# Gathers queued in two parts around the gate matrix, and low halves in two GpSimd instructions

## The chip, the cores and the metric

The kernel runs on one core of a Trainium2 chip. The metric is the device time of one execution in microseconds (us). The engines are called PE (TensorE, with PEld for its weight loads), DVE (VectorE), ACT (ScalarE), POOL (GpSimd) and SP (SyncE, which issues plain DMAs here). Each engine works through its own queue in order. A line number such as L820 is the line of the kernel before.

## What is computed

One decoder layer over 1024 tokens of width 1024, all in float32: a norm, one combined projection, three token mixers merged by gates (the mixer), and then a feed-forward part in which every token chooses 128 of 16384 experts. Only that last part is touched by the gathers:

```python
def peer_ffn(xn, w_peer_q, peer_keys, peer_u, peer_v):      # per block of tokens
    sc = jnp.einsum('thid,hikd->thik', q, peer_keys)         # scores for two halves of the key
    top_v, top_i = lax.top_k(sc, PEER_TOPK)
    ...
    eid = jnp.take_along_axis(cidx, best_pos, axis=-1)       # 8 heads x 16 experts for each token
    gate = jax.nn.softmax(best_v, axis=-1)
    u = peer_u[eid]
    act = jax.nn.gelu(jnp.einsum('thkd,td->thk', u, xt))
    v = peer_v[eid]
    return jnp.einsum('thk,thkd->td', gate * act, v)
x = x + peer_ffn(rms_norm(x, ln_ffn))                        # then a final norm
```

## The kernel before

**Tiling.** Tokens lie on 128 partitions. The 1024 tokens go in three blocks (`BLOCKS`): 256, 512 and 256. `mixer` is a generator for one block; while block b finishes, the first steps of block b+1 run between, and `routing` (which finds `eid` and `gate`) of block b runs beside them. For the middle block the experts are computed densely (`dense`, with `gate_matrix` making a 512 x 16384 matrix of gates from one-hot `quad` tiles, `g_d`). For the other two blocks, four tiles of 128 tokens, the experts' rows are fetched: `gathered` issues for each tile 128 gathers from `u` and 128 from `v`, 1024 in all. A gather (L820) is an indirect DMA, issued by GpSimd, of 128 rows of 4 KB into a buffer `g4{k % 7}`; VectorE then multiplies a `u` row tile with the tokens and sums (L830, result in `dots`), or adds a weighted `v` row tile to the output rows in PSUM (L837).

**Weights.** Every weight tile of 128 x 1024 goes through `unit`: SP loads `raw`, ScalarE rounds it to `whi` (L164), and GpSimd, for some units VectorE, makes the rest `wlo = raw - whi` (L165, in `split`). TensorE then multiplies three times (`mm3`, L191 to L193). So a unit is 24 matmuls and one subtraction.

**Order.** The program text is traced once, and a planner then orders each engine's instructions by priority and by a timeline of its own, before the run; the order is fixed on the chip. Buffers of one name (`tag`) are handed out in the order of the program text. `unit` notes in `marks` its priority, its ScalarE and GpSimd instructions and a rate. `pace` turns the rates into due times: `due` adds up the rates, a slot of due time is two gathers, and the gather takes the priority of its unit (`cur_priority`) and is queued on GpSimd behind that unit's subtraction (`issue_after`, L819). The rates are 1.0 and 0.3 in the first and second routing (`RATE_ROUTING`), 1.5 and 0.5 in the mixers behind them (`RATE_MIXER`), 0.5 from the last routing on (`RATE_LAST`), and 0 from the dense stage on; there the gathers that are left are spread evenly over the dense units.

**Buffers.** There are seven gather buffers (`NG`, tags `g40` to `g46`). `gate_matrix` takes its quads from three of them, tags `g44` to `g46` (L856), and one more use of `g46`. While the gate matrix is made, `slots` lets gathers use only the other four (`NQ_GATHER`). The loop that traces all gathers (`for t in range(TT)`, at the end of `layer_kernel`) comes last in the program text.

Of the kernel before, what the change touches and what calls it, by code (L numbers as in the profile page):

```python
# [8 lines left out]
F32 = mybir.dt.float32  # L9
# [5 lines left out]
ALU = mybir.AluOpType  # L15
# [3 lines left out]
D = 1024  # L19
# [3 lines left out]
TT = T // P  # L23
# [13 lines left out]
SLOTS = HEADS * TOPK  # L37
# [6 lines left out]
NG = 7  # L44
# [6 lines left out]
NQ_GATHER = 4  # L51
# [12 lines left out]
def layer_kernel(ctx, tc, a, out_d):  # L64
    nc = tc.nc
# [97 lines left out]
    def split(hi, lo, src, eng=None):  # L163
        return (nc.scalar.copy(hi, src),  # L164
                (eng or nc.vector).tensor_tensor(lo, src, hi.bitcast(F32), op=ALU.subtract))  # L165

    marks, rate = [], [0.0]
# [3 lines left out]
    def unit(src, n=D, k=KD):  # L171
        prio = tc.cur_priority
        if in_mix[0] and len(marks) % 4 == 3:
            raw = tmp.tile([P, D], F32, tag="raw4", name="raw", bufs=1)
        else:
            raw = wts.tile([P, D], F32, tag="raw", name="raw")
        dst = raw[:, :n]
        if len(src.shape) == 3:
            dst = dst.rearrange("p (k c) -> p k c", k=src.shape[1])
        nc.sync.dma_start(dst, src)  # L180
        hi = wts.tile([P, D], F32R, tag="whi", name="whi")
        lo = wts.tile([P, D], F32R, tag="wlo", name="wlo")
        share[0] += lo_dve[0]
        on_dve = share[0] >= 1
        share[0] -= on_dve
        first, second = split(hi[:, :n], lo[:, :n], raw[:, :n], nc.vector if on_dve else nc.gpsimd)
        marks.append((prio, first, marks[-1][2] if on_dve and marks else second, rate[0]))
        return (hi[:, :n].rearrange("p (k c) -> p k c", k=k), lo[:, :n].rearrange("p (k c) -> p k c", k=k))

# [613 lines left out]
    def held(src):  # L803

        stage = gat.tile([P, D], F32, tag="held", name="stage", bufs=1)
        nc.sync.dma_start(stage, src)
        ps = psum.tile([P, D], F32, tag="row", name="row_ps", bufs=1)
        nc.scalar.copy(ps, stage)
        return ps

    def gathered(tt, eid, gt, pace, slots):

        def rows_of(table, k, half):
            n = tt * SLOTS + (half * SLOTS + k) / 2
            m0, m1 = pace(n), pace(n, LAG)
            if m0:
                tc.cur_priority = m0[0]
            g = gat.tile([P, D], F32, tag=f"g4{k % slots(n)}", name="g4", bufs=1)
            with (tc.issue_after(m0[2].ins) if m0 else nullcontext()):  # L819
                nc.gpsimd.indirect_dma_start(out=g, out_offset=None, in_=a[table],  # L820
                                             in_offset=bass.IndirectOffsetOnAxis(ap=eid[:, k:k + 1], axis=0))
            if m0:
                tc.cur_priority = m1[0]
            return g, m1

        xn = held(xn_d[tt * P:(tt + 1) * P, :])
        w = gat.tile([P, SLOTS], F32, tag="dots", name="dots", bufs=2)
        for k in range(SLOTS):
            g, m1 = rows_of("u", k, 0)
            nc.vector.scalar_tensor_tensor(g, g, 1.0, xn, op0=ALU.mult, op1=ALU.mult, accum_out=col(w, k))  # L830
        with (tc.issue_after(m1[1].ins) if m1 else nullcontext()):
            nc.scalar.activation(w, w, AF.Gelu_apprx_tanh)
        nc.vector.tensor_tensor(w, w, gt, op=ALU.mult)
        acc = held(x2_d[ROW0[tt]:ROW0[tt] + P, :])
        for k in range(SLOTS):
            g, _ = rows_of("v", k, 1)
            nc.vector.scalar_tensor_tensor(acc, g, col(w, k), acc, op0=ALU.mult, op1=ALU.add)  # L837
        final_rows(tt, acc)
# [125 lines left out]
    eid = gat.tile([P, TT, SLOTS], I32, tag="eid", name="eid", bufs=1)  # L964
# [13 lines left out]
    def fill(count, dp=None):  # L978
        for _ in range(count):
            if todo:  # L980
                i, n = todo.pop(0)
                act = d2(dp) if dp else tmp.tile([P, T], F32, tag="sp", name="sp", bufs=2)
                nc.sync.dma_start(act_d[n], dense_act(i, held_xT[0], None, act, mm_ps()))

    mT = mem_norm()
    x_sb = x_norm(0)
    mem_kv(mT)
    now = mixer(0, x_turn(x_sb, PK_LN_MIX))
    for b in range(1, len(BLOCKS)):
# [6 lines left out]
        shared = []  # L996
# [31 lines left out]
        for _ in range(chunks):  # L1028
            until(nxt, "chunk")
            spill(KD // chunks)  # L1030
    m_gate = len(marks)
    quads = gate_matrix(ij_dense, gate_dense)
    gates_done = False
    for label in now:
# [8 lines left out]
                pass  # L1043
        elif not isinstance(label, str):
            xnT = label
    m_gathers = len(marks)
    rate[0] = RATE_LAST
    routing(xnT, b16()[:, 0:2048], gate[:, 2:4], eid[:, 2:4], beside=lambda: fill(FILL_ROUTING[1]))
    mix.close()
# [7 lines left out]
    dense(BLOCKS[DENSE][0], held_xT[0], dp, acts)  # L1057
    m_last = len(marks)


    units = marks[m_dense:m_last]
    at = [n for n, m in enumerate(marks) if m[3] > 0]
    early_units = [marks[n] for n in at]
    due, total = [], 0.0
    for m in early_units:
        due.append(total)
        total += m[3]
    n1 = int(total)

    def pace(n, lag=0):  # L1070
        if n < n1:
            return early_units[bisect_right(due, min(n + lag * .5, due[-1])) - 1]
        return units[min(int((n - n1) * len(units) / (TT * SLOTS - n1)) + lag, len(units) - 1)]

    def slots(n):

        shared = n < n1 and m_gate <= at[bisect_right(due, n) - 1] < m_gathers
        return NQ_GATHER if shared else NG

    for t in range(TT):  # L1080
        gathered(t, eid[:, t], gate[:, t], pace, slots)


_OUTS = [((1, 1024, 1024), 'float32')]
# [63 lines left out]
```

## Time and profile before

| | |
|---|---|
| median of 3 runs | 4071.53 us (4069.44 to 4078.17) |
| the profiled execution | 4092.4 us, span 4090.7 us |
| busy: PE, DVE, ACT, POOL | 3233.4, 2930.3, 1471.6, 2583.4 us (79%, 72%, 36%, 63% of the span) |
| mean granted clock of PE | 0.903 of full speed |
| gathers | 1024, of 0.996 us each on POOL in the mean |
| HBM | 951.86 MB read, 70.25 MB written |

Busy shares are means over stages with different limits, so the page's forty slices are read first and then tables by stage. For the tables I cut the span at the times at which the work changes: first routing and the middle block's mixer (513 to 1210 us), second routing (to 1480), gate matrix (to 1830), rest of the third block's mixer with the last routing (to 2340), dense stage (to 3484), and what is behind it.

### The profile page before, as it was taken

To read this page: it belongs to the slowest core of one execution; us is meant where nothing else is said; L and a number is where in the kernel's file an instruction comes from. 1 tells how busy PE (TensorE), PEld (TensorE's weight loads), DVE (VectorE), ACT (ScalarE), POOL (GpSimd) and SP (SyncE) were. 2 spreads that over 40 slices of the span, in tenths; PEclk is the share of its full clock that TensorE was granted. 3 is DMA by queue.
4 is the path that set the end of the run, shared out by engine and by line. 5 is a ranking of instruction groups with operands and counts; after the bars stand their busy time and mean duration, and the time that the engine had idled before them with its cause. 6 is when DMAs were issued, how large, how long until landed. Compare 5 with 4: busy or idle time off the path is not lost. (4 is left out here: it accounts for less than half of the span.)

```text
span 4090.7 us, 49506 instructions
## 1 busy us (share of the span) xinstructions
PE 3233.4 (79%) x16928; PEld 2735.3 (67%) x16928; DVE 2930.3 (72%) x5354; ACT 1471.6 (36%) x2201; POOL 2583.4 (63%) x1897
## 2 busy tenths in 40 slices
PE   7899999999999998888788999999999999000000
PEld 7799788888778887877677777777877877000000
DVE  3532576432439985666699788887888878898889
ACT  5555456342345557774333232322322322000000
POOL 6586566225234466778877767666666677676665
PEclk9999999999999999999899999999999999555555
DMA  5254453234233344569977999989999998999998
GB/s 193 99 200 160 164 175 118 78 111 141 96 127 135 132 135 165 207 223 350 348 267 251 326 326 335 334 308 335 326 325 330 332 334 316 370 396 363 376 369 349
DMA packets 360349, 1025.40 MB, mean 251 GB/s; under 512 B 33312, under 2 KB 118688, under 8 KB 357664
## 3 DMA queue, kind: packets, MB, share of 16 engines
q0 software_dynamic: 147456, 536.94, 35.2%
q1 hardware_dynamic: 212640, 485.31, 34.0%
q8 instruction: 133, 2.18, 0.2%
q14 instruction: 120, 0.98, 0.1%
HBM read 951.86 MB, written 70.25 MB: 250 GB/s over the span
## 5 line engine op out<-in xcount | busy, mean ns | idle before, releaser
L165 POOL TENSOR_TENSOR wlo<-raw,whi 128x1024 fp32r<-128x1024 f32 x521 | 1258.6, 2421 | 591.0 <-ACT whi L164 536.9
L164 ACT CAST whi<-raw 128x1024 fp32r<-128x1024 f32 (+1 forms) x623 | 647.5, 1044 | 1012.0 <-PE mm_ps L193 366.9
L193 PE MATMUL mm_ps<-a,wlo 128*128 128x256 f32 (+1 forms) x2808 | 939.6, 337 | 42.7 <-POOL wlo L165 40.1
L191 PE MATMUL mm_ps<-a,whi 128*128 128x256 f32 (+1 forms) x2808 | 946.7, 340 | 24.6 <-ACT whi L164 12.9
L192 PE MATMUL mm_ps<-a,whi 128*128 128x256 f32 (+1 forms) x2808 | 942.9, 337 | 1.0 <-DVE a L165 0.9
L820 POOL DMA_INDIRECT g<-in_u_dram,eid x512 | 509.8, 996 | 306.8 <-DVE g L830 162.4
L837 DVE SCALAR_TENSOR_TENSOR row_ps<-g,dots,row_ps 128x1024 f32<-128x1024 f32 x512 | 658.9, 1287 | 47.1 <-DMA g<-in_v_dram,eid 31.9
L820 POOL DMA_INDIRECT g<-in_v_dram,eid x512 | 509.9, 996 | 283.8 <-DVE row_ps L837 142.0
L830 DVE SCALAR_TENSOR_TENSOR g<-g,row_ps 128x1024 f32<-128x1024 f32 x512 | 610.9, 1214 | 63.3 <-DMA g<-in_u_dram,eid 49.0
L193 PEld LDWEIGHTS mm_ps<-a,wlo 128*128 128x128 f32 x2808 | 539.1, 192 | 102.6 <-POOL wlo L165 47.4
L191 PEld LDWEIGHTS mm_ps<-a,whi 128*128 128x128 f32 x2808 | 539.7, 193 | 82.6 <-ACT whi L164 16.2
L192 PEld LDWEIGHTS mm_ps<-a,whi 128*128 128x128 f32 x2808 | 540.9, 193 | 53.3 <-DVE a L165 1.6
L192 PE MATMUL mm_ps<-wlo,d 128*128 128x512 f32 x1024 | 411.5, 402 | 12.8 <-POOL wlo L165 12.2
L193 PE MATMUL mm_ps<-whi,d 128*128 128x512 f32 x1024 | 407.6, 400 | 0.3 <-DVE d L165 0.3
L191 PE MATMUL mm_ps<-whi,d 128*128 128x512 f32 x1024 | 378.7, 399 | 10.2 <-DVE a L945 8.0
L192 PEld LDWEIGHTS mm_ps<-wlo,d 128*128 128x128 f32 x1024 | 195.6, 191 | 64.5 <-POOL wlo L165 16.8
L191 PEld LDWEIGHTS mm_ps<-whi,d 128*128 128x128 f32 x1024 | 193.8, 189 | 62.4 <-DVE a L945 8.8
L165 DVE TENSOR_TENSOR wlo<-raw,whi 128x1024 fp32r<-128x1024 f32 (+1 forms) x102 | 151.6, 1486 | 116.3 <-ACT whi L164 111.5
L193 PEld LDWEIGHTS mm_ps<-whi,d 128*128 128x128 f32 x1024 | 195.7, 191 | 47.1 <-DVE d L165 0.7
L191 PE MATMUL tp_ps<-a,whi 128*128 128x512 f32 x512 | 200.9, 392 | 5.5 <-ACT whi L164 5.5
L193 PE MATMUL tp_ps<-a,wlo 128*128 128x512 f32 x512 | 201.3, 393 | 2.0 <-POOL wlo L165 2.0
L192 PE MATMUL tp_ps<-a,whi 128*128 128x512 f32 x512 | 200.6, 392 | 0.0
(296 smaller groups left out, 4791.6 us busy)
## 6 DMA issues: line engine op xcount, KB each, us to landing
raw<-in_win_a_dram SPq DMA_DIRECT2D x156, 512.0 KB
raw<-in_uT_a_dram SPq DMA_DIRECT2D x128, 512.0 KB
raw<-in_v_b_dram SPq DMA_DIRECT2D x128, 512.0 KB
raw<-in_br_a_dram SPq DMA_DIRECT2D x72, 512.0 KB
g_d<-b SPq DMA_DIRECT2D x16, 2048.0 KB
a<-g_d SPq DMA_DIRECT2D x32, 1024.0 KB
raw<-in_win_b_dram SPq DMA_DIRECT2D x48, 512.0 KB
raw<-in_pq_a_dram SPq DMA_DIRECT2D x48, 512.0 KB
```

The source lines that it names most:

```text
L164: return (nc.scalar.copy(hi, src), (eng or nc.vector).tensor_tensor(lo, src, hi.bitcast(F32), op=ALU.subtract))
L165: (eng or nc.vector).tensor_tensor(lo, src, hi.bitcast(F32), op=ALU.subtract))
L191: nc.tensor.matmul(ps, lhsT=l_hi, rhs=r_hi, start=start, stop=False)
L192: nc.tensor.matmul(ps, lhsT=l_hi, rhs=r_lo, start=False, stop=False)
L193: nc.tensor.matmul(ps, lhsT=l_lo, rhs=r_hi, start=False, stop=stop)
L820: nc.gpsimd.indirect_dma_start(out=g, out_offset=None, in_=a[table], in_offset=bass.IndirectOffsetOnAxis(ap=eid[:, k:k + 1], axis=0))
L830: nc.vector.scalar_tensor_tensor(g, g, 1.0, xn, op0=ALU.mult, op1=ALU.mult, accum_out=col(w, k))
L837: nc.vector.scalar_tensor_tensor(acc, g, col(w, k), acc, op0=ALU.mult, op1=ALU.add)
```

## The change

Two things are changed. First, the gathers become one generator, `gathers`, which runs over all four tiles and yields the due time of its next gather. `queue_gathers()` is called once just ahead of `gate_matrix` and traces the gathers that are due up to there; a second call, `queue_gathers(last=True)`, at the end traces the others. The due times, priorities and the rule of `issue_after` stay; from the second part on, `slots` gives four buffers up to the end of the rated units, where it gave four only while the gate matrix and its mixer ran. Second, where GpSimd makes the low half of a full unit, it does so in two instructions of 512 columns; the ScalarE instruction stays whole, and `marks` notes the second of the two.

```diff
@@ unit
-        first, second = split(hi[:, :n], lo[:, :n], raw[:, :n], nc.vector if on_dve else nc.gpsimd)
+        if on_dve or n < D:
+            first, second = split(hi[:, :n], lo[:, :n], raw[:, :n], nc.vector if on_dve else nc.gpsimd)
+        else:
+            first = nc.scalar.copy(hi, raw)
+            for h in (slice(0, n // 2), slice(n // 2, n)):
+                second = nc.gpsimd.tensor_tensor(lo[:, h], raw[:, h], hi[:, h].bitcast(F32), op=ALU.subtract)
@@ gathered
-    def gathered(tt, eid, gt, pace, slots):
+    def gathered(tt, eid, gt):
+        def slot(k, half):
+            return tt * SLOTS + (half * SLOTS + k) / 2
...
+        yield slot(0, 0)
         xn = held(xn_d[tt * P:(tt + 1) * P, :])
         w = gat.tile([P, SLOTS], F32, tag="dots", name="dots", bufs=2)
         for k in range(SLOTS):
+            yield slot(k, 0)
             g, m1 = rows_of("u", k, 0)
...
         for k in range(SLOTS):
+            yield slot(k, 1)
             g, _ = rows_of("v", k, 1)
@@ layer_kernel
+    due, early_units, units = [0.0], [], []
+    def pace(n, lag=0):
+        if n < due[-1]:
+            return early_units[bisect_right(due, min(n + lag * .5, due[-2])) - 1]
+        n0 = due[-1]
+        return units[min(int((n - n0) * len(units) / (TT * SLOTS - n0)) + lag, len(units) - 1)]
+    def slots(n):
+        return NQ_GATHER if due[-1] > n >= n_gate[0] else NG
+    def all_gathers():
+        for t in range(TT):
+            yield from gathered(t, eid[:, t], gate[:, t])
+    gathers, n_next, n_gate = all_gathers(), [0], [TT * SLOTS]
+    seen = [0]
+    def queue_gathers(last=False):
+        for m in marks[seen[0]:]:
+            if m[3] > 0:
+                early_units.append(m)
+                due.append(due[-1] + m[3])
+        seen[0] = len(marks)
+        if last:
+            units.extend(marks[m_dense:m_last])
+        prio = tc.cur_priority
+        while n_next[0] is not None and (last or n_next[0] < due[-1] - 1):
+            n_next[0] = next(gathers, None)
+        tc.cur_priority = prio
...
-    m_gate = len(marks)
+    queue_gathers()
+    n_gate[0] = n_next[0]
     quads = gate_matrix(ij_dense, gate_dense)
...
-    for t in range(TT):
-        gathered(t, eid[:, t], gate[:, t], pace, slots)
+    queue_gathers(last=True)
```

## Rows read from the trace of the kernel before

**Rows 1.** The page's forty slices: busy tenths of two engines.

```profile
PE   7899999999999998888788999999999999000000
DVE  3532576432439985666699788887888878898889
```

**Rows 2.** Busy time of every engine by stage, with granted clock, DMA share, GB/s.

```profile
core 0: us, PE busy (x) PEld busy (x) DVE busy (x) ACT busy (x) POOL busy (x), PEclk, DMA share, GB/s
513.00:1210.00 697.00, 678.34 (x3360) 562.83 (x3359) 329.03 (x846) 299.07 (x477) 296.74 (x166) 1.00 0.35 122
1210.00:1480.00 270.00, 260.19 (x1472) 225.95 (x1471) 256.25 (x1003) 145.38 (x191) 124.50 (x68) 0.98 0.39 129
1480.00:1830.00 350.00, 305.73 (x2206) 283.50 (x2205) 230.19 (x407) 250.63 (x411) 248.47 (x207) 0.97 0.50 184
1830.00:2340.00 510.00, 423.45 (x2126) 358.99 (x2124) 413.35 (x944) 175.10 (x256) 391.69 (x296) 0.91 0.87 308
2340.00:3484.00 1144.00, 1106.07 (x4679) 886.01 (x4678) 957.80 (x1145) 322.62 (x421) 786.69 (x565) 0.99 0.92 328
3484.00:4090.70 606.70, 0.00 (x0) 0.00 (x0) 543.39 (x617) 11.43 (x16) 392.03 (x418) 0.50 0.96 371
```

**Rows 3.** The same stages, gathers alone (L820 on POOL; x is their count).

```profile
513.00:1210.00 697.00, 7.77 (x8) 1.00 0.35 122
...
1480.00:1830.00 350.00, 1.35 (x2) 0.97 0.50 184
1830.00:2340.00 510.00, 164.52 (x171) 0.91 0.87 308
2340.00:3484.00 1144.00, 454.06 (x427) 0.99 0.92 328
3484.00:4090.70 606.70, 392.03 (x418) 0.50 0.96 371
```

**Rows 4.** POOL in order of time: start, us, operation, idle time before it.

```profile
512.99 1.13 POOL L820 DMA_INDIRECT g<-in_u_dram,eid  x1 [1.63 <-DVE carry L314]
...
528.75 0.96 POOL L820 DMA_INDIRECT g<-in_u_dram,eid  x1 [0.15 <-issue]
...
1827.37 0.83 POOL L864 TENSOR_TENSOR quad<-quad,tr 128x384 f32<-128x384 f32 x1 [0.37 <-DVE quad L860]
1828.34 1.00 POOL L820 DMA_INDIRECT g<-in_u_dram,eid  x1
```

**Rows 5.** Groups by form: VectorE's work on gathered rows (busy us, mean ns).

```profile
L837 DVE SCALAR_TENSOR_TENSOR row_ps<-g,dots,row_ps 128x1024 f32<-128x1024 f32 x512 | 658.9, 1287 | 47.1 <-DMA g<-in_v_dram,eid 31.9 <-issue 2.5
L830 DVE SCALAR_TENSOR_TENSOR g<-g,row_ps 128x1024 f32<-128x1024 f32 x512 | 610.9, 1214 | 63.3 <-DMA g<-in_u_dram,eid 49.0 <-ACT row_ps L808 5.3 <-DVE g L830 1.8
L830 DVE DVE_READ_ACCUMULATOR g<-g,row_ps 128x1 f32 x512 | 41.2, 81 | 0.0
```

**Rows 6.** Groups by form: GpSimd's two-input operations of three widths.

```profile
L165 POOL TENSOR_TENSOR wlo<-raw,whi 128x1024 fp32r<-128x1024 f32 x519 | 1257.7, 2428 | 579.3 <-ACT whi L164 525.1 <-PE mm_ps L193 30.5 <-issue 8.9
...
L529 POOL TENSOR_TENSOR b<-b,t 128x512 f32<-128x512 f32 x16 | 23.3, 1461 | 57.5 <-DVE t L528 30.5 <-DVE rs_s L155 27.0
...
L165 POOL TENSOR_TENSOR wlo<-raw,whi 128x128 fp32r<-128x128 f32 x2 | 0.9, 474 | 11.8 <-ACT whi L164 11.8
```

**Rows 7.** All engines in order of time, two instructions of the second routing.

```profile
1403.17 2.41 POOL L165 TENSOR_TENSOR wlo<-raw,whi 128x1024 fp32r<-128x1024 f32 x1 [1.39 <-ACT whi L164]
...
1403.53 2.11 DVE L733 TENSOR_TENSOR b<-topv 128x48 f32<-128x48 f32 x1
```

**Rows 8.** Groups by form, VectorE in the dense stage.

```profile
L912 DVE TENSOR_TENSOR d<-d,a 128x512 f32<-128x512 f32 x124 | 133.6, 1083 | 75.2 <-ACT d L960 45.2 <-DMA d<-act_d 28.4 <-issue 1.4
L165 DVE TENSOR_TENSOR d<-d,d 128x512 fp32r<-128x512 f32 x128 | 126.3, 995 | 19.4 <-PE mm_ps L192 14.9 <-ACT d L164 2.5 <-ACT whi L164 1.5
L945 DVE TENSOR_TENSOR a<-a,mm_ps 128x512 f32<-128x512 f32 x176 | 116.0, 682 | 40.9 <-PE mm_ps L193 38.6 <-PE tp_ps L193 1.8
```

**Rows 9.** Waits in the dense stage: who waited for whom, us, times, longest.

```profile
POOL g L820 <- DVE row_ps L837: 113.1, 91, 7.7
POOL g L820 <- DVE g L830: 111.2, 93, 4.2
```

More of the change, by code (lines that the diff above doesn't have):

```diff
@@ L809, in held @@
         return ps
-    def gathered(tt, eid, gt, pace, slots):
+    def gathered(tt, eid, gt):
+        def slot(k, half):
+            return tt * SLOTS + (half * SLOTS + k) / 2
         def rows_of(table, k, half):
-            n = tt * SLOTS + (half * SLOTS + k) / 2
+            n = slot(k, half)
             m0, m1 = pace(n), pace(n, LAG)
@@ L1045, in layer_kernel @@
             xnT = label
-    m_gathers = len(marks)
     rate[0] = RATE_LAST
@@ L1058, in layer_kernel @@
     m_last = len(marks)
[L1061 to L1078, printed above, removed]
-    for t in range(TT):
-        gathered(t, eid[:, t], gate[:, t], pace, slots)
+    queue_gathers(last=True)
 _OUTS = [((1, 1024, 1024), 'float32')]
```

## The prediction

> **What bounds the kernel now.** I read the page's forty slices first. PE is at 7 to 9 tenths up to slice 34 and at 0 in the last six, while DVE stays at 8 or 9 to the end [rows 1]. So two regimes follow each other: a long one in which TensorE works, and a tail without it. The table of stages puts the border at 3484 us: TensorE is busy 1106.07 of 1144 us in the dense stage before it, and not at all in the 606.70 us behind it [rows 2]. The same table for L820 alone counts the gathers: the tail issues 418 of the 1024, or 606.70 / 418 = 1.45 us for each [rows 3]. What sets the end is thus how many gathers are left when the dense stage is over.
>
> Then I asked why so many are left. The kernel plans otherwise. Each weight unit (one call of `unit`) carries a rate in `marks`, and `pace` makes rate x 2 gathers due beside it. Counting units in the program text: 41 at 1.0 in the first routing, 76 at 1.5 in the middle block's mixer (8 + 48 + 16 + 4), 57 at 0.3 in the second routing, 8 at 0.5. That is 41 + 114 + 17.1 + 4 = 176.1 due slots, or 351 gathers before the gate matrix (the loop stops one slot short). From there to the dense stage come about 74 + 40 + 14 units at 0.5, another 64 slots. So 480 gathers should be out when the dense stage begins, and 544 are to be spread over its 192 units. The trace has 8 up to 1210 us, 2 more by 1830 and 171 more by 2340: 181, not 480 [rows 3].
>
> The cause stands in the queue of GpSimd. Eight gathers go out from 512.99 to 528.75 us, and the next at 1828.34, just behind the last `quad` multiplication [rows 4]. Gather k writes buffer `g4{k % 7}`, and `gate_matrix` takes buffers 4 to 6 for its quads. The quads come earlier in the program text than all gathers, so gathers 4, 5 and 6 get their buffers only when the last quad is through. Gathers 0 to 3 and 7 to 10 use buffers 0 to 3 and do get out: eight. VectorE takes them in order, so 7 to 10 then hold their buffers until 4 to 6 have come. For 1300 us no gather moves, beside a VectorE that is busy only 329.03 of 697 us in the first of these stretches [rows 2].
>
> **Part one: gathers queued in two parts.** It removes no gather. It puts the 351 that are due before the gate matrix ahead of the quads in the program text, so they no longer wait for them; the quads now wait for these.
>
> The tail. If the plan holds, 480 are out at the start of the dense stage. The dense stage issued 427 while every gather was overdue [rows 3], so I take this as what the planned order can pack into it, not as what was asked of it. GpSimd waited there 113.1 + 111.2 us for VectorE to free a buffer [rows 9]. Left over: 544 - 427 = 117, less 17 that part two may add (below): 100, at 1.45 us 145 us. The bounds: 0 left if the dense stage takes all 544 (its VectorE is idle 1144 - 957.80 = 186 us, and 117 x 1.29 = 151 would fit), or 150 if the plan is 33 behind at its start, 218 us. I take 100, since 427 is the nearest row.
>
> At this place the skill speaks against the upper hope. The row first: the dense stage moves 328 GB/s at a DMA share of 0.92, the tail 371 at 0.96 [rows 2]. 117 more gathers of 128 x 4 KB in 1144 us are 54 GB/s, 382 in all. The Trainium skill, "DMA: Bandwidth & Descriptors", Specifications, gives about 358 GB/s as the HBM limit of one core. By that limit the dense stage has room for 30 GB/s, an estimate of 65 gathers, and the tail would keep 52 of them, some 75 us. The trace does not agree with the figure, as its tail ran at 371.
>
> What the gathers cost where they go. One takes VectorE 1.214 us and 0.081 for its sum (u), or 1.287 (v) [rows 5], so 1.29. From 513 to 1210 us, 82 + 228 are due where 8 went: 302 x 1.29 = 390 us on top of 329.03 makes 719 us in a stage of 697, in which TensorE is busy 678.34 [rows 2]. At 100% of VectorE that is +22; at the 84% that it reached in the dense stage (957.80 / 1144) it is 719 / 0.84 - 697 = +159. I take +60. In the second routing VectorE is already the bound: 256.25 of 270 us [rows 2]. 34 gathers add 44: 300 - 270 = +30 at most beyond its idle time, 0 if part two gives it back; I take +20. From 1480 to 1830, 45 more make 230.19 + 58 = 288 of 350: cover enough, 0. The fourth stage gets relief, since about 84 gathers are due where 171 went: 87 x 1.29 = 112 us off VectorE's 413.35 of 510, in a stage where TensorE is idle 86.55 us [rows 2]. Bounds 0 and -87; I take -30. Sum of these stages: +50, between -60 and +200.
>
> Queues moved past: on GpSimd each gather is an instruction of about 1.0 us [rows 4] among the low halves; 302 x 1.0 + 296.74 = 599 of 697 us leaves cover [rows 2]. On SP only eight row loads and four row stores move; four loads go early, and SP would hold weight loads behind one that waits. ScalarE's gelu of `dots` comes once per 128 gathers. I cost both at nothing, and at 10 us if that cover is gone.
>
> **Part two: low halves in two instructions.** GpSimd's 1024-column subtraction takes 2428 ns and the 128-column one 474 [rows 6], so 195 + 2.18 per column: 512 columns 1312, a pair 2624, +0.2 us. The other bound is a GpSimd multiplication of 512 columns at 1461 [rows 6]: a pair 2922, +0.5. I take 0.2, the same operation. For 519 units it is 102 us of GpSimd, 28 of them in the dense stage, where it is idle 1144 - 786.69 = 357 [rows 2]: hidden, 0; without that cover up to +28 there.
>
> What it may give: VectorE waits out GpSimd's subtraction. At 1403.53 a 128x48 addition took 2.11 us and ended at 1405.64, where the subtraction begun at 1403.17 ended too (1405.58) [rows 7]. In the dense stage L912 (two SBUF inputs) takes 1083 ns, L945 of the same size with one input in PSUM 682; L165 on `d` takes 995 [rows 8]. That is 0.40 x 124 + 0.31 x 128 = 90 us of waiting. This agrees with the Trainium skill, "SBUF — State Buffer", Who interferes with whom: the pair of ports is held for a whole instruction, and the other engine fully blocks. By that rule an instruction half as long blocks half as long. From the rows: 45 us of VectorE come free in the dense stage, or 35 gathers at 1.29; I count half of them, 17, since the order of the queues is laid down before the run. TensorE also gets the first half of each `wlo` 1.1 us sooner; with its stalls on `wlo` spread thin I count 0.
>
> **The sum.** 4090.7 (span) - 606.7 + 145 + 50 = 3679; with the 1.7 us around the span (4092.4 - 4090.7) 3681. The profiled execution stands 0.5% above the median of the runs (4071.53 / 4092.4 = 0.995): 3662, so **3660**.
>
> **Rivals.**
> (a) The dense stage takes all 544 and the stages before cost nothing: 3484 + 30 for the last gathers and rows = 3514, median 3495. For it speak the 186 us of idle VectorE; against it the 427 and the DMA share of 0.92. Chance 0.14.
> (b) VectorE becomes the bound from 513 to 1480 and the quads, now behind the gathers on buffers 4 to 6, come late: +200 and 150 left: 3484 + 200 + 218 = 3902, median 3880. For it speaks 719 of 697; against it that in the dense stage 38 gathers per 100 us went beside a TensorE at 97%. Chance 0.18.
> (c) The change doesn't do what it says: something else holds the early gathers (the one PSUM row buffer, `eid`). The first eight ran while later heads of `eid` were still being written, which speaks against. 4070. Chance 0.02.
> (d) Slower: the quads wait for the last of the 351, and with them the stage buffers that the third block's mixer needs, so that TensorE stands still. The gain to lose is 437 - 50 us. 351 gathers at the fourth stage's 171 / 510 us take 1047 us from 513, until 1560: 80 us late. It turns the sign only if they run at under 0.24 per us, so that the gate matrix starts after 1970 us. Then the time is above 4080, say 4150. Chance 0.04.
> The forecast itself: 0.62, with its own range 3540 to 3800.
>
> **How the numbers follow.** About 0.2% is what a measurement of this kernel can tell from no change. Faster: 0.62 + 0.14 + 0.18 = 0.94; same 0.02; slower 0.04. The range reaches from the middle of (a) and the forecast's low end to the lower part of (b): 3525 to 3840.
>
> **What would show it.** Right: gathers from 513 us on without a gap, about 310 by 1210 and 480 at the dense stage's start; a tail of 50 to 150 gathers; `wlo` on GpSimd as twice as many instructions of about 1.3 us, and L912 nearer to 0.9 than 1.08. Wrong: still a gap in L820 before the quads (c); TensorE under 85% from 513 to 1480 with VectorE near 100% (b, d); a tail under 30 gathers (a).

## The result, and the profile after

| | before, same chip | after |
|---|---|---|
| median | 4070.53 us | 3787.74 us (3784.82 to 3790.39) |
| ratio to before | 1 | 0.9301 [0.9285, 0.9317] |
| the profiled execution | | 3790.39 us, span 3788.7 us |
| mean granted clock of PE | 0.903 | 0.933 |

The change takes 7.0% off. The forecast was 3660 with a range of 3525 to 3840: the sign and the range held, and the time came out 128 us above the forecast. Lines have moved: the gather L820 is now L829, VectorE's work on `u` and `v` rows L841 and L849, the low half L191 (its ScalarE cast L189), the quads L872 (VectorE), L876 (GpSimd) and L882 (TensorE), L912 is L924.

The page's forty slices, PE and DVE, against [rows 1]:

```profile
PE   7999987799999898977777989999999999999910
DVE  2521479997889799976665469877887988887799
```

The tail without TensorE has shrunk from six slices to two. In exchange PE now has slices at 7 early (7, 8) and around the gate matrix (18 to 22), where it mostly had 8 or 9, and DVE is at 7 to 9 from slice 6 to 18, where it had mostly 2 to 6.

To compare the same work in two traces, a cut by time does not serve, since all stages have moved. I number the 623 casts `whi<-raw` of ScalarE, which come in the same order in every kernel here, and cut at the same seven of them. Counted from the two traces:

```
stage (same units)                  before us  after us  differs  gathers before, after
first routing                           168.0     236.1    +68.1      7,  72
mixer of the middle block               538.2     589.5    +51.3      0, 237
second routing                          254.1     277.5    +23.4      0,  34
gate matrix                             361.4     455.6    +94.1      3,  51
rest of third mixer, last routing       506.1     428.2    -77.9    170,  85
dense stage                            1119.5    1102.1    -17.4    413, 423
last unit to the end                    630.0     193.9   -436.1    430, 121
```

The table of busy time by stage, cut at these units in the trace of after, and the same for the gathers alone; both answer to [rows 2, 3]. The columns are those of [rows 2].

```profile
506.00:742.00 236.00, 176.44 (x910) 151.61 (x909) 220.68 (x678) 98.82 (x140) 172.89 (x170) 0.88 0.74 252
742.00:1331.00 589.00, 542.23 (x2499) 437.32 (x2499) 495.36 (x651) 213.75 (x352) 437.70 (x385) 0.96 0.87 314
1331.00:1609.00 278.00, 250.25 (x1400) 218.03 (x1399) 275.05 (x1050) 143.97 (x188) 160.04 (x135) 0.94 0.56 189
1609.00:2064.00 455.00, 351.06 (x2272) 325.80 (x2271) 305.68 (x532) 259.48 (x414) 311.69 (x312) 0.86 0.57 207
2064.00:2493.00 429.00, 394.28 (x2087) 336.56 (x2087) 282.42 (x731) 171.91 (x252) 324.91 (x295) 0.97 0.75 257
2493.00:3595.00 1102.00, 1079.65 (x4610) 868.21 (x4610) 918.63 (x1162) 314.15 (x405) 800.42 (x693) 0.99 0.94 338
3595.00:3788.00 193.00, 16.43 (x71) 12.91 (x69) 179.37 (x158) 9.27 (x22) 116.89 (x124) 0.55 0.90 349
```

```profile
506.00:742.00 236.00, 69.58 (x73) 0.88 0.74 252
742.00:1331.00 589.00, 247.27 (x238) 0.96 0.87 314
...
2493.00:3595.00 1102.00, 447.48 (x423) 0.99 0.94 338
3595.00:3788.00 193.00, 114.13 (x121) 0.55 0.90 349
```

The gap in the gathers is gone. Up to the first routing's start one had been issued, then 72, 237, 34, 51 and 85 more: 480 when the dense stage begins, to the number. In the first two rows VectorE is busy 220.68 of 236 and 495.36 of 589 us; in the second routing 275.05 of 278. The gate matrix is the odd one: no engine is near its limit there, and yet it took 94 us more than before.

The waits of the gate matrix's stage, after and then before, same units (who waited for whom: us, times, longest):

```profile
PEld mm_ps L882 <- POOL quad L876: 81.8, 34, 6.6
...
POOL quad L876 <- DVE quad L872: 76.8, 78, 4.5
...
DVE g L841 <- DMA g<-in_u_dram,eid: 53.3, 14, 9.6
...
DVE row_ps L849 <- DMA g<-in_v_dram,eid: 14.3, 10, 3.4
```

```profile
POOL quad L864 <- DVE quad L860: 51.8, 76, 4.1
PEld mm_ps L870 <- POOL quad L864: 37.6, 31, 4.3
```

Read from below: VectorE waits 67.6 us in all for gathered rows to land, where before it had no such wait here, GpSimd waits longer for VectorE's `quad` step (76.8 against 51.8), and TensorE for GpSimd's (81.8 against 37.6). One such place in order of time, first GpSimd, then VectorE:

```profile
1651.49 2.55 POOL L191 TENSOR_TENSOR wlo<-raw,whi 128x512 fp32r<-128x512 f32 x2 [5.69 <-ACT whi L189]
1654.18 0.98 POOL L829 DMA_INDIRECT g<-in_u_dram,eid  x1
```

```profile
1649.48 1.88 DVE L446 TENSOR_TENSOR b<-b,tp_ps 128x512 f32<-128x512 f32 x3
1660.62 1.22 DVE L841 SCALAR_TENSOR_TENSOR g<-g,row_ps 128x1024 f32<-128x1024 f32 x1 [9.26 <-DMA g<-in_u_dram,eid]
```

The gather is queued behind a low half that waited 5.69 us for its cast. It goes out at 1654.18. VectorE, whose queue is in order too, has reached the multiplication on that row tile at 1651.36 and stands there for 9.26 us with everything that is queued behind it.

### The profile page after: what moved, and what is told of

The parts are those of the page before. It is cut to its first block, busy times and chain, and to the rows that moved or that the text cites. A ratio compares the mean times of both kernels' runs of the same rounds, so it can differ in the third digit from the quotient of the medians.

```text
span 3788.7 us, 50038 instructions
## 1 busy us (share of the span) xinstructions
PE 3272.9 (86%) x16928; PEld 2772.3 (73%) x16928; DVE 2853.4 (75%) x5354; ACT 1478.9 (39%) x2203; POOL 2687.0 (71%) x2416
## 3 DMA queue, kind: packets, MB, share of 16 engines
q14 instruction: 124, 1.02, 0.1%
## 5 line engine op out<-in xcount | busy, mean ns | idle before, releaser
L191 POOL TENSOR_TENSOR wlo<-raw,whi 128x512 fp32r<-128x512 f32 x1038 | 1340.7, 1317 | 380.7 <-ACT whi L189 370.2
L189 ACT CAST whi<-raw 128x1024 fp32r<-128x1024 f32 x519 | 542.5, 1048 | 830.8 <-PE mm_ps L198 353.8
L849 DVE SCALAR_TENSOR_TENSOR row_ps<-g,dots,row_ps 128x1024 f32<-128x1024 f32 x512 | 658.1, 1285 | 119.9 <-DMA g<-in_v_dram,eid 111.1
L829 POOL DMA_INDIRECT g<-in_u_dram,eid x512 | 528.5, 1032 | 253.9 <-DVE g L841 137.7
L829 POOL DMA_INDIRECT g<-in_v_dram,eid x512 | 517.9, 1012 | 215.5 <-DVE row_ps L849 130.8
L841 DVE SCALAR_TENSOR_TENSOR g<-g,row_ps 128x1024 f32<-128x1024 f32 x512 | 607.3, 1209 | 68.7 <-DMA g<-in_u_dram,eid 67.7
L198 PE MATMUL mm_ps<-whi,d 128*128 128x512 f32 x1024 | 403.6, 396 | 0.0
L196 PE MATMUL mm_ps<-whi,d 128*128 128x512 f32 x1024 | 368.1, 398 | 8.9 <-DVE a L957 6.4
L882 PE MATMUL mm_ps<-quad 128*128 128x128 f32 x1024 | 164.8, 330 | 77.0 <-POOL quad L876 74.8
L882 PEld LDWEIGHTS mm_ps<-quad 128*128 128x128 f32 x1024 | 156.0, 241 | 85.5 <-POOL quad L876 81.8
L196 PE MATMUL tp_ps<-a,whi 128*128 128x512 f32 x512 | 201.5, 394 | 7.0 <-ACT whi L189 4.7
```

Of the source, the lines that this page charges most:

```text
L189: first = nc.scalar.copy(hi, raw)
L191: second = nc.gpsimd.tensor_tensor(lo[:, h], raw[:, h], hi[:, h].bitcast(F32), op=ALU.subtract)
L196: nc.tensor.matmul(ps, lhsT=l_hi, rhs=r_hi, start=start, stop=False)
L198: nc.tensor.matmul(ps, lhsT=l_lo, rhs=r_hi, start=False, stop=stop)
L882: nc.tensor.matmul(ps[:, u * P:(u + 1) * P], lhsT=oj[:, u, :], rhs=oi[:, u, :], start=True, stop=True)
```

## The experiments

Each ratio is to the kernel before on the same chip. Stage times are by the same units as in the table above.

**Part one alone.** The low half is one instruction again.

```diff
-        if on_dve or n < D:
...
-            for h in (slice(0, n // 2), slice(n // 2, n)):
-                second = nc.gpsimd.tensor_tensor(lo[:, h], raw[:, h], hi[:, h].bitcast(F32), op=ALU.subtract)
+        first, second = split(hi[:, :n], lo[:, :n], raw[:, :n], nc.vector if on_dve else nc.gpsimd)
```

> Part one alone: the gathers are queued in two parts, the low halves stay in one GpSimd instruction. Theory (the order alone makes the gain): 3790 us, between 3760 and 3820; 480 gathers out at the start of the dense stage, some 120 left behind it. Rival (the shorter subtractions are what lets the gathers in between the units): 3850 or more, with 30 or more gathers further behind at the end of the dense stage, and L924 back at 1.08 us instead of 1.05.

Measured: 3806.26 us, ratio 0.9308 [0.9293, 0.9324]. Stages 234, 600, 283, 445, 425 and 1103 us, 480 gathers out at the dense stage's start, 121 in the tail. That is the first reading. The second reading's sign came out the other way round: without the halves the instruction of L924 (L919 here) took 1.01 us in the dense stage, with them 1.04.

**Part two alone.** The kernel before, with its loop over all gathers at the end of the text, and the low half in two instructions.

> Part two alone: the loop of gathers stays at the end as before. Theory (the halves are worth little by themselves): 4070 us, between 4050 and 4090. Rival (VectorE's waits for GpSimd's port fall by half, 45 us in the dense stage, and with them the tail by 35 gathers): 4020 or less. Second rival (two starts for each unit cost GpSimd 100 us that are not hidden): 4100 or more.

Measured: 4067.13 us, ratio 0.9940 [0.9923, 0.9956]; the second routing took 243 us (254 before), the gate matrix 373 (361), the dense stage 1123 (1120). The two together: nearly all of the gain is that of the order of the gathers. The halves give 0.6% by themselves. What they give beside part one is between nothing and about 0.5%. The ratios 0.9301 and 0.9308 agree, but they come from chips on which the kernel before took 4071 and 4092 us; on a chip where it took 4090, the later-use kernel below, whose stages are those of the changed one, has 0.9256. The next kernel ran on the chip of part one alone and has the halves and the same gathers up to the gate matrix: it gets there at 1615 us, part one alone at 1633. In the gate matrix itself part one alone is the shorter, 445 us against 448 to 456 in the kernels with halves.

**No gathers beside the gate matrix.** The rate is 0 there, and higher from the last routing on.

```diff
-RATE_LAST = 0.5
+RATE_LAST = 1.18
@@ after queue_gathers()
+    rate[0] = 0
     quads = gate_matrix(ij_dense, gate_dense)
```

> The changed kernel, but units traced beside the gate matrix carry rate 0, and the last routing's rate goes from 0.5 to 1.18, so that the same 480 gathers are due before the dense stage. Theory (the gate matrix's stage took 456 us instead of 361 since VectorE stands at gathers that haven't landed): the stage falls back to 370 or less, while the last routing, with some 50 gathers more, gets 30 to 60 us longer; 3720 to 3770 in all. Rival (the quads are slower for another reason: the halves, or the block's later start): the stage stays at 430 or more and the time is 3790 or more.

Measured: 3815.37 us, ratio 0.9320 [0.9305, 0.9336]. The stage fell from 456 to 387 us with 9 gathers in it in place of 51. Its waits:

```profile
POOL quad L876 <- DVE quad L872: 60.1, 81, 4.5
PEld mm_ps L882 <- POOL quad L876: 42.7, 36, 4.5
...
DVE g L841 <- DMA g<-in_u_dram,eid: 18.1, 2, 9.9
```

So 42 gathers cost that stage 69 us, and with them went 50 of the 68 us of waits for landing. The total that the first reading gave, 3720 to 3770, was missed. The kernel is not faster for it: the next stage, with four buffers, issued 83 gathers in 455 us (85 in 428), 436 were out at the dense stage's start, and the tail grew to 169.

**Fewer gathers in the first routing.**

```diff
-RATE_ROUTING, RATE_MIXER = (1.0, 0.3), (1.5, 0.5)
-RATE_LAST = 0.5
+RATE_ROUTING, RATE_MIXER = (0.3, 0.3), (1.5, 0.5)
+RATE_LAST = 1.03
```

> The changed kernel, but the first routing's rate is 0.3 instead of 1.0 (58 gathers fewer there) and the last routing's 1.03 instead of 0.5. Theory (VectorE, asked for more than there is time in the first routing, is what made that stage 236 us instead of 168): the stage falls to 185 or less; what the 58 gathers cost in the last routing, where VectorE has time, is under 40 us; 3740 to 3775 in all. Rival (the time was lost to GpSimd's queue or to DMA and follows the gathers wherever they go): the last routing grows by as much as the first shrinks, 3790 within 15.

Measured: 3825.25 us, ratio 0.9352 [0.9337, 0.9368]. The first routing took 180 us with 26 gathers. With 7 gathers it was 168, with 72 it was 236: from 0.6 to 1.2 us for each one more. The stage came out as the first reading had it, the total as neither. What came free was paid behind: the stage before the dense one took 463 us with 112 gathers, and 154 were left for the tail.

**Seven buffers behind the gate matrix.** The kernel of the third experiment, where gathers due from the last routing on use seven buffers.

```diff
     def slots(n):
-        return NQ_GATHER if due[-1] > n >= n_gate[0] else NG
+        return NQ_GATHER if n_gate[1] > n >= n_gate[0] else NG
...
+    n_gate[1] = sum(m[3] for m in marks)
     rate[0] = RATE_LAST
```

> As the run without gathers beside the gate matrix (rate 0 there, 1.18 in the last routing), but from the last routing on the gathers use seven buffers again instead of four. Theory (four buffers are what kept that stage at 83 gathers though 136 were due): 120 or more gathers in the last routing, 480 out at the start of the dense stage, a tail of 125 or fewer; the last routing grows by up to 45 us; 3755 to 3800 on the chip where the kernel before took 4092, where the changed kernel would take 3806 (0.930). Rival (VectorE, busy in the routing, is what limits that stage): still under 95 gathers and the time of the run with four, 3815 within 12.

Measured: 3817.42 us, ratio 0.9330 [0.9304, 0.9356]: 102 gathers in 469 us in place of 83 in 455, 455 out at the dense stage's start. In gathers that is a miss for both readings, in time it is the rival's: three more buffers moved 19 gathers, not all that were due, and brought no time.

**Eight and six buffers in the dense stage.** An eighth buffer is taken from room that is free behind the last mixer; in the other kernel the dense stage's gathers use six.

```diff
     def slots(n):
+        if n >= due[-1]:
+            return NG + 1
...
```

```diff
     def slots(n):
+        if n >= due[-1]:
+            return NG - 1
...
```

> The changed kernel with an eighth gather buffer in the dense stage and behind it. Theory (the buffers set how many gathers the dense stage takes: 423 with seven): about 470, a tail of 75 instead of 121, 60 to 75 us less: ratio 0.912 to 0.917. Rival (DMA at a share of 0.92, or VectorE, is the limit): 423 within 12, ratio 0.930 within 0.003, or TensorE's dense stage 20 us longer or more.

> The changed kernel with six gather buffers in the dense stage and behind it. Theory (buffers are the limit): about 370 gathers in the dense stage, a tail of 170 to 180, 75 to 100 us more: ratio 0.948 to 0.956. Rival (another limit): 423 within 12 and a ratio under 0.936.

Measured: 3781.09 us, ratio 0.9239 [0.9208, 0.9270] with eight; 3787.23 us, 0.9259 [0.9233, 0.9285] with six. The dense stage of the two, eight first:

```profile
2494.00:3669.00 1175.00, 1104.55 (x4609) 875.02 (x4608) 997.21 (x1223) 312.37 (x404) 852.49 (x751) 0.98 0.95 344
```

```profile
2494.00:3569.00 1075.00, 1070.74 (x4616) 866.00 (x4615) 897.41 (x1128) 315.07 (x403) 784.29 (x673) 1.00 0.94 337
```

With six, seven and eight buffers the stage issued 403, 423 and 482 gathers and took 1075, 1102 and 1175 us; the tail kept 141, 121 and 62. From the stage's start to the end it is 1291, 1296 and 1284 us. So a gather that the dense stage takes costs it (1175 - 1075) / (482 - 403) = 1.3 us, and spares the tail (217 - 109) / (141 - 62) = 1.4. Each reading had half of it: the buffers do set how many gathers the stage takes, as the first says, and taking more makes the stage longer and the kernel no faster, as the rival says. With six buffers TensorE is busy 1070.74 of 1075 us, so the stage can't be shorter than that; what is packed in beyond lengthens it.

**VectorE takes a row later.** The distance between a gather and its use is five units, not two.

```diff
-LAG = 2
+LAG = 5
```

> The changed kernel with LAG 5 instead of 2: VectorE's work on a gathered row is queued three units later behind the gather's issue. Theory (in the gate matrix's stage VectorE stood 68 us at rows that hadn't landed, and that is most of the 94 us by which the stage grew): the waits fall under 25 us and the stage from 456 to 410 or less; buffers are held longer, so the dense stage may take up to 40 gathers fewer; ratio 0.920 to 0.945. Rival (the gathers' own instructions between the quads make the stage long): the waits fall, the stage stays at 440 or more.

Measured: 3783.74 us, ratio 0.9256 [0.9227, 0.9284]; the gate matrix took 448 us, with waits for landing of 51.6 + 6.8 us. Hardly anything moved: VectorE's instructions come in the same order up to the gate matrix, and in it 461 of 490 stand at the same place, so the experiment doesn't tell what the waits alone cost.

**Half of VectorE's work on the rows, then half of the bytes too.** In the first, gathers stay whole and VectorE works on 512 of the 1024 columns, for `u` as for `v`, so half of every sum is left out; in the second, gathers also fetch rows of 2 KB (by the same indices in a table of twice as many rows, so not halves of the same experts).

```diff
-nc.vector.scalar_tensor_tensor(acc, g, col(w, k), acc, op0=ALU.mult, op1=ALU.add)
+nc.vector.scalar_tensor_tensor(acc[:, 0:512], g[:, 0:512], col(w, k), acc[:, 0:512], op0=ALU.mult, op1=ALU.add)
...
-nc.gpsimd.indirect_dma_start(out=g, out_offset=None, in_=a[table],
+nc.gpsimd.indirect_dma_start(out=g[:, 0:512], out_offset=None, in_=a[table].rearrange("r (h c) -> (r h) c", h=2),
```

> The changed kernel, but VectorE works on 512 of a gathered row's 1024 columns (the other half of the sums is left out); the gathers move whole rows as before. From the dense stage's start to the end the changed kernel and the runs with six, seven and eight buffers all took 1284 to 1296 us. Theory (the DMA of the gathered rows and weights, some 434 MB in that time, sets it): still 1230 or more. VectorE's share of what the earlier stages lost comes back: the first routing takes 200 us or less instead of 236, the middle block's mixer 575 or less; ratio 0.895 to 0.915. Rival (VectorE sets dense stage and tail too): 1190 or less from the dense stage's start, ratio under 0.89.

> As the run with half of VectorE's work, and the gathers move rows of 2 KB instead of 4 KB too (the first halves of a table's rows by another index; outputs are not the reference's). Theory (DMA sets dense stage and tail): with 142 MB less the stage is TensorE's own again: 1120 to 1170 us from the dense stage's start to the end, fewer than 60 gathers behind it; ratio 0.855 to 0.88. Rival (the order laid down before the run, or GpSimd's one microsecond for each gather, sets it): within 30 us of the run with whole rows.

Measured: 3724.05 us, ratio 0.9110 [0.9096, 0.9124], and 3635.34 us, 0.8889 [0.8875, 0.8902]. First the kernel with VectorE's half (gate matrix, dense stage, and 100 us of its tail), then the one with half rows (first routing, dense stage):

```profile
1574.00:2019.00 445.00, 342.61 (x2283) 317.37 (x2282) 286.79 (x531) 261.73 (x418) 311.43 (x310) 0.89 0.58 211
...
2451.00:3545.00 1094.00, 1077.35 (x4611) 865.79 (x4610) 714.10 (x1172) 315.37 (x404) 790.26 (x699) 1.00 0.95 344
...
3600.00:3700.00 100.00, 0.00 (x0) 0.00 (x0) 58.15 (x77) 0.00 (x0) 72.10 (x78) 0.50 1.02 404
```

```profile
503.00:738.00 235.00, 184.62 (x913) 156.21 (x912) 192.95 (x717) 95.21 (x139) 182.65 (x181) 0.88 0.56 186
2463.00:3601.00 1138.00, 1091.53 (x4609) 875.56 (x4608) 781.42 (x1281) 313.53 (x404) 911.02 (x809) 0.98 0.76 257
```

From the dense stage's start to the end: 1296 us in the changed kernel, 1269 with half of VectorE's work, 1170 with half of the bytes as well, with 5 gathers left for the tail. The DMA share goes 0.94, 0.95, 0.76. So half of VectorE's work is worth 27 us there and half of the bytes 99 more, together with whatever a shorter transfer changes in the planned order. The first routing hardly answers: 236, 226 and 234 us (72, 80 and 83 gathers), although VectorE's 220.68 of 236 fell to 192.95 of 235 and the DMA share to 0.56. This is the miss in both runs, and with it the second's total: 0.8889 where 0.855 to 0.88 was expected. The mixer took 572 and 592 us (589). The gate matrix took 444 and 439 us; VectorE still waits for landing in both (the first two views), and for less of it in part one alone (the third):

```profile
DVE g L841 <- DMA g<-in_u_dram,eid: 43.7, 15, 9.2
...
DVE row_ps L850 <- DMA g<-in_v_dram,eid: 12.7, 10, 3.1
```

```profile
DVE g L841 <- DMA g<-in_u_dram,eid: 55.6, 16, 9.6
...
DVE row_ps L850 <- DMA g<-in_v_dram,eid: 23.5, 11, 4.3
```

```profile
DVE g L836 <- DMA g<-in_u_dram,eid: 27.2, 13, 8.1
...
DVE row_ps L844 <- DMA g<-in_v_dram,eid: 10.0, 8, 2.2
```

Halving the instructions took 11 of the 94 us, so VectorE's own work on the rows is the smaller part of the price in that stage. That waiting for landing is the larger part isn't shown: with 37, 56, 68 and 79 us of such waits (part one alone, half of VectorE's work, the change, half rows) the stage took 445, 444, 456 and 439.

**Two attempts at a better order.** The first has no gathers beside the gate matrix, then seven buffers at a rate of 1.3, `RATE_LAST` 0.8, and eight buffers in the dense stage. The second adds less in the first routing and more in the mixer.

```diff
@@ the first
-RATE_LAST = 0.5
+RATE_LAST = 0.8
...
+    rate[0] = 0
     quads = gate_matrix(ij_dense, gate_dense)
...
+            n_gate[1] = sum(m[3] for m in marks)
+            rate[0] = 1.3
@@ the second, on top of the first
-RATE_ROUTING, RATE_MIXER = (1.0, 0.3), (1.5, 0.5)
+RATE_ROUTING, RATE_MIXER = (0.5, 0.3), (1.8, 0.5)
```

> A version meant to be faster: the changed kernel with no gathers due beside the gate matrix, rate 1.3 from its end to the last routing and 0.8 in it, seven buffers there and eight in the dense stage. Theory (a gather costs 1.6 us beside the gate matrix, 0.9 between it and the dense stage, 1.3 in the dense stage, 1.5 behind it): gate matrix 387 us, the stage behind it 490, 500 gathers out at the dense stage's start, 40 us less than the changed kernel: ratio 0.915 to 0.922. Rival (what is taken from one stage is paid in the next, since DMA and VectorE are full from there on): 0.926 to 0.933.

> The run with seven buffers behind the gate matrix and eight in the dense stage (ratio 0.925), with the first routing's rate down from 1.0 to 0.5 and the middle block's mixer up from 1.5 to 1.8: some 40 gathers go from a stage where one cost about 1 us to one where 237 cost 57 us. Theory (the mixer has room for more at that price): first routing 195 us, mixer 605 or less, as many gathers out at the dense stage's start: ratio 0.915 to 0.921. Rival (the mixer is full at 0.40 gathers for each us, with DMA at a share of 0.9): it grows by 40 us or more, or the gathers fall behind; 0.924 or more.

Measured: 3780.77 us, ratio 0.9249 [0.9237, 0.9262], and 3782.82 us, 0.9273 [0.9256, 0.9290]. In the first the gate matrix took 387 us (-69), the stage behind it 505 (+77, with 140 gathers), the dense stage 1171 (+69, with 476), and what follows 100 (-94). That total lies between the two readings. In the second the first routing fell to 190 us with 40 gathers, but the mixer took 244 at a rate of 1.8 where it had taken 237 at 1.5, and the others slid into the second routing: 64 there, 320 us in place of 278, and the total is the rival's. The kernel before took 4091 and 4079 us on these chips, longer than the 4070.53 beside the changed kernel; the later-use kernel, whose stages are those of the changed one, had 0.9256 against 4090 us. Beside that, neither of the two, nor eight buffers at 0.9239, is told apart from the change.

## Why the prediction was right, and where it missed

The sum was 3679 us for the span, and 3788.7 came out: 110 more. By its terms, from the table of stages:

| term | counted | measured | misses by |
|---|---|---|---|
| first routing and mixer | +60 | +68 + 51 = +119 | 59 |
| second routing | +20 | +23 | 3 |
| gate matrix | 0 | +94 | 94 |
| stage behind it | -30 | -78 | -48 |
| dense stage | 0 | -17 | -17 |
| the tail | -606.7 + 145 = -462 | -436 | 26 |

(The first routing also began 7 us earlier, which closes the sum.)

**What bounded the kernel: right.** The gathers waited for buffers that the quads held in the program text's order. With the order of the text changed, 480 were out at the dense stage's start, as counted from the rates, and 121 left at its end, where 100 were counted. (By the prediction's own border, the end of TensorE's work, 117 and 177 us were left.) The first experiment shows that this part alone carries nearly all of the gain.

**The first stages: the work was right, the size off.** The working had VectorE's 719 us, a bound of +22 at full use and +159 at the 84% of the dense stage, and then took +60, which is nearest to no row. By the same units VectorE's work is 220.68 + 495.36 = 716 us, in 825 us (87%). From 513 to 1210, where the prediction looked, it is 88.5%:

```profile
513.00:1210.00 697.00, 609.23 (x2878) 499.31 (x2879) 616.99 (x1171) 268.35 (x418) 521.51 (x476) 0.94 0.83 295
```

719 / 0.885 - 697 is +115, and +119 was measured, but the 0.885 is known only afterwards: neither bound gives the number. The two halves of this stretch differ, though: 65 more gathers cost the first routing 68 us, 237 cost the mixer 51. Since half of the work and half of the bytes left the first routing at 226 and 234 us, "VectorE is full" isn't the whole reason there. It follows the number of gathers queued (180 us with 26); what beside them holds it stays open.

**The gate matrix: the step that failed.** "Cover enough, 0" compared busy sums, 288 of 350 us. The sum was even close (VectorE is busy 305.68 us there now), but it says nothing of waits in an in-order queue. A gather is issued behind a unit's low half; where that unit comes late, VectorE stands at the row's multiplication, the quads behind it come late, and TensorE waits for them. With the gathers out, 69 of the 94 us came back, 50 of the 68 us of landing waits with them, and the waits for the quads fell to 60.1 and 42.7 us, near the 51.8 and 37.6 of before; with VectorE's instructions half as long, 11 us came back. Some 12 us more are the halves': part two alone took 373 us in this stage, and the working counted nothing for that. Set beside its own gather in the trace, each of VectorE's 24 waits splits: of 67.5 us, 13.9 pass before the gather is issued, 3.9 while GpSimd issues it, and 49.7 from there to its landing. Yet the stage does not grow with these waits, as the experiments with half of the work show. Shown is that these gathers cost the stage 69 us and that their instructions' length is the smaller part; how the rest divides between landing and the place in the queue stays open, since the later use hardly changed the order. TensorE itself is slower there: the same matmuls (2274 and 2272) were busy 316.73 us before and are 351.06 now, at a granted clock of 0.97 and 0.86, means between its two levels of 2.4 and 1.2 GHz. With the gathers out it is 327.34 us at 0.93, so most of this goes with the gathers. The stage of before:

```profile
1474.00:1835.00 361.00, 316.73 (x2274) 293.48 (x2273) 236.61 (x423) 253.87 (x414) 254.62 (x211) 0.97 0.50 184
```

**The stage behind: right in kind, larger.** Relief from 170 to 85 gathers was worth 78 us, 0.92 each, inside the bounds of 0 and -87. It nearly pays for the gate matrix: the two together are +16, where -30 was counted.

**The dense stage and the tail: the number held, the reason did not.** The 427 was read as what the order can pack, with cover for more if more could be packed. Six, seven and eight buffers show that more can be packed (482) and that each costs the stage 1.3 us. From the dense stage's start the kernel pays for 544 gathers, wherever they go: 1284 to 1296 us. Rival (a), all 544 inside at no cost, is excluded by that price. That bytes are the larger part of what is paid for there is what half rows speak for (99 us beyond the 27 of VectorE's half), less cleanly than the rest, because with them the order also put 539 gathers in the stage. What the prediction took from the Trainium skill, "DMA: Bandwidth & Descriptors", Specifications, can be judged here. By its 358 GB/s the tail would have kept 52 gathers; it kept 121 at 338 GB/s in the stage, so neither that figure nor the free cover set the number. The Trainium skill, "HBM Reference", Specifications (TRN2), adds that a core streaming alone measures well above that share, about 425 GB/s; the 404 GB/s in 100 us of the tail with half of VectorE's work agree with it.

**Part two: the cost right, the gain not there.** The pair costs what was worked out, 2 x 1317 ns where 2 x 1312 was counted (the operation at 1461 ns, taken as the other bound, is an addition and not a multiplication; nothing hung on it):

```profile
L191 POOL TENSOR_TENSOR wlo<-raw,whi 128x512 fp32r<-128x512 f32 x1038 | 1340.7, 1317 | 380.7 <-ACT whi L189 370.2
```

VectorE in the dense stage (of after, against [rows 8]; the one line of before that is not shown there, and part one alone, without halves):

```profile
L924 DVE TENSOR_TENSOR d<-d,a 128x512 f32<-128x512 f32 x124 | 128.5, 1040 | 85.8 <-ACT d L972 80.8 <-DMA d<-act_d 4.6
L165 DVE TENSOR_TENSOR d<-d,d 128x512 fp32r<-128x512 f32 x128 | 112.7, 889 | 16.2 <-PE mm_ps L197 13.2 <-ACT d L164 2.3
...
L165 DVE TENSOR_TENSOR wlo<-raw,whi 128x1024 fp32r<-128x1024 f32 x57 | 95.6, 1677 | 31.5 <-ACT whi L164 31.5
```

```profile
L165 DVE TENSOR_TENSOR wlo<-raw,whi 128x1024 fp32r<-128x1024 f32 x57 | 89.7, 1574 | 17.1 <-ACT whi L164 12.3 <-issue 4.7
```

```profile
L165 DVE TENSOR_TENSOR d<-d,d 128x512 fp32r<-128x512 f32 x128 | 129.3, 1017 | 20.6 <-PE mm_ps L192 10.0 <-ACT d L164 9.1 <-ACT whi L164 0.7
L919 DVE TENSOR_TENSOR d<-d,a 128x512 f32<-128x512 f32 x124 | 124.1, 1007 | 98.1 <-ACT d L967 73.3 <-issue 17.5 <-DMA d<-act_d 5.0
...
L165 DVE TENSOR_TENSOR wlo<-raw,whi 128x1024 fp32r<-128x1024 f32 x57 | 85.9, 1508 | 6.3 <-ACT whi L164 5.7 <-issue 0.5
```

Against before, L924 fell by 43 ns, L165 on `d` by 106, and L165 on `wlo` rose by 103: 5.3 + 13.6 - 5.9 = 13 us, where 45 were worked out. But these 13 are not shown to come from the halves. Against part one alone, the halves make L924 33 ns longer, L165 on `d` 128 shorter and on `wlo` 169 longer: 16.4 - 4.1 - 9.7, under 3 us. Part two alone has 1155, 1020 and 1602 ns, all longer than before, and among the kernels with halves L924 runs from 0.95 to 1.19 us. L924 was to come near 0.9 us and stands at 1.04. With and without the halves the dense stage issued 423 gathers: of the 17 that were counted for part two none came, and that term is wrong, though a small one.

**Rivals.** (b) was nearest in its mechanism: from 506 to 1609 us VectorE is busy 991.09 of 1103 us, 90%, and TensorE 968.92, 88%, just above the 85% named as its sign. Its price was nearer too: the stages ahead of the dense one took 119 + 23 + 94 - 78 = +158 us, where (b) had +200 and the forecast +50. The measured 3788 us lie 128 above the forecast and 92 below (b). They stay inside the forecast's own range up to 3800 because 121 gathers were left and not 150, and because the stage behind the gate matrix gave back 48 us more than was counted and the dense stage 17. Nothing in the working foresaw that these would cover part of the 156 us lost in the three stages ahead of them; that much of the hit is luck. (d) did not come: the first quad ran at 1667.8 us. Its own bound was mis-summed: the gain to lose is 462 - 50 = 412 us by the forecast's tail, not 437 - 50, so the sign would have turned at 1480 + 412 = 1892 us and not at 1970.

## What to carry to other kernels

Where buffers are handed out in the order of the program text, a transfer that is planned early but written late in the text waits for whoever is written before it: a stretch without that transfer, beside an engine that is half idle, is its sign. Cover is not a sum of busy time: before work is moved into an in-order queue, look at what will arrive late there and who stands behind it. And when moving the same transfers from stage to stage leaves the end where it was, count their price per stage (here 0.2 us in the mixer and 0.6 to 1.6 in the others) and look at their bytes, not at their order.

## What the runs showed of the hardware

An operation cut in two on GpSimd does not halve what VectorE waits: in the dense stage VectorE's three operations beside it took 1040, 889 and 1677 ns with the halves, and 1007, 1017 and 1508 without. VectorE's L924 beside a pair of halves, twice (L924, then the pair of the same place):

```profile
2472.51 1.39 DVE L924 TENSOR_TENSOR d<-d,a 128x512 f32<-128x512 f32 x1 [1.91 <-ACT d L972]
...
2505.15 3.64 DVE L924 TENSOR_TENSOR d<-d,a 128x512 f32<-128x512 f32 x1 [1.23 <-ACT d L972]
```

```profile
2472.06 2.98 POOL L191 TENSOR_TENSOR wlo<-raw,whi 128x512 fp32r<-128x512 f32 x2 [1.80 <-ACT whi L189]
...
2505.67 2.55 POOL L191 TENSOR_TENSOR wlo<-raw,whi 128x512 fp32r<-128x512 f32 x2
```

At 2472.51 VectorE ended at 2473.90, inside the pair, which ends at 2475.04 and took 2.98 us instead of 2.55: VectorE got in between the halves, and GpSimd paid 0.43 us. At 2505.15 it ended at 2508.79, behind both halves (2508.22), in 3.64 us. The Trainium skill, "SBUF — State Buffer", Who interferes with whom, says that a VectorE instruction with two inputs in SBUF contends with a GpSimd instruction that reads SBUF, and that issue order decides who blocks. (That the pair of ports is held for a whole instruction, as the prediction has it, the section says of VectorE's two-port modes.) The first place agrees with that; the second shows that the gap between two halves is not always taken.

Gathers alone, with VectorE at half work, ran at 404 GB/s and a DMA share of 1.02 (78 in 100 us); over the dense stage, beside the weights, no kernel here came above 346.
